# A two-layer hybrid decoder step: layer 1's rotations made in layer 0, short caches copied by sequence, load buffers by last use

## The chip, the cores and the metric

The kernel runs on 1 core of one Trainium2 chip. The metric is the device time of one execution in microseconds (us), lower is better. Before the change it is 2431.61 us, the median of 3 runs (2431.44 to 2434.77).

## The reference, cut to what matters

The reference is one inference step of two layers for a prompt of 512 positions and 8 sample sequences of 8 positions (T = 576 columns in all), with a model width of 1024, in float32. In each layer one projection of the normed input feeds four token mixers: A, dilated sliding-window attention in three head groups with caches of 128, 512 and 2048 positions (a1, a2, a3); B, grouped-query attention with a cache of 128 positions (b); C, a gated short convolution; D, a complex diagonal state-space layer. Their gated sum is projected, and a feed-forward part and a per-layer embedding follow. The outputs include the caches of the samples moved on by 8 positions, so that the old part of each cache is copied.

```python
a_bar = jnp.exp(lam * dt)                       # one complex number per state: a size and an angle
bu = jnp.einsum('blgi,gni->blgn', uf.astype(jnp.complex64), b_bar)
_, xs = lax.associative_scan(_ssm_combine, (a_seq, bu), axis=1)
y = jnp.einsum('blgn,gin->blgi', xs, c_mat).real + lp['ssm_d'].astype(f32) * uf
...
fk = jnp.concatenate([cache[2 * g].astype(ka.dtype), ka[:, :, g]], axis=1)
new += [last_rows(fk, lb), last_rows(fv, lb)]
```

## The kernel before, in words

Activations lie with channels on the 128 partitions and the 576 columns in two halves of 288. Each weight block of 128x512 (636 in all, 318 a layer, in the order of use) is loaded by SP's queue into one of 4 raw buffers (`wr`, `load_blk`, line 612), rounded by ScalarE to a high part (`wh`) and completed by GpSimd to a low part (`wl`, `split_blk`, line 617); 8 split blocks are held (NSPL, line 286). `gemms` (line 681) makes each product of three matmuls, so a block gives 4 x 2 x 3 = 24 matmuls of 128x288.

The program is written out by a planner in Python: `Build.track` (line 382) keeps a clock for each engine by its own costs, and every step of the main path lets side tasks (generators) go on when the planner thinks their inputs are there. The side tasks run in streams: state space, transposes of values, attention B, attention A, caches of the samples. The result is one fixed order for each engine, and each engine takes its instructions in order. The constants of this planner stand per layer in `PACE` (line 276): CALM is how far VectorE's clock may be ahead before a side task waits, BATCH after how many pieces side tasks are looked at, CONC how many tasks of a stream run at a time, PRE how many cache tiles are loaded ahead, MARGIN how many buffers stay free. Activations, loads and temporary data share 63 buffers of one size: `slot` (line 553) takes the one that was given back first, `drop` (line 558) gives it back. All profiled instructions bear line 256, that of the recording helper.

All transfers are issued by SP. The old cache parts are copied from DRAM to DRAM (`copies`, line 916; `after_step`, line 950, issues them evenly by count over the program): a1 in pieces of 2 sequences, a2 in halves of a sequence, a3 in eighths, b in pieces of 4 sequences (`COPY_PIECES`, line 33).

The state space has 8 blocks of 128 states. Its scan is made in real numbers: the input is turned back by the angle of its position, scanned with the size alone, and turned forward. The cosines and sines for 256 positions are doubled from 32: `ssm_setup` (line 1143) makes the 32 for all blocks and the output weights `ck`; `ssm_pair` (line 1464) loads the input weights (`bT`) and the inputs (`uscr`, a scratch in DRAM) of 2 blocks, doubles their 32 to 256 with 20 VectorE instructions, and scans two chunks of 256 positions. For layer 1, `ssm_setup` runs in layer 0's last steps. `sa_task` (line 1932) goes through the caches of 4 samples in 13 chunks, with tiles that `prefetch` (line 1959) loads ahead.

Of the kernel before, what the change touches and what calls it, by code (L numbers as in the profile page):

```python
# [19 lines left out]
L = 2  # L20
# [12 lines left out]
COPY_PIECES = {"a1": (2, 1), "a2": (1, 2), "a3": (1, 8), "b": (4, 1)}  # L33
# [234 lines left out]
def _free(ap):  # L268
    n = 1
    for st, c in list(ap.ap)[1:]:  # L270
# [6 lines left out]
    dict(CALM=5.12, ACALM=1.89, RES=4, LOBIAS=7.86, SLACK=-0.07, SIDE_MAX=4, MARGIN=0, PRE=6,  # L277
         CONC=(1, 3, 1, 2, 2), XCALM=0.3, SQP=-0.3, NEAR=-0.03, SCALM=4.55, SN=3, HOLD=False, BATCH=3, GR=2),
    dict(CALM=1.41, ACALM=0.0, RES=1, LOBIAS=14, SLACK=0.21, SIDE_MAX=3, MARGIN=3, PRE=8,
         CONC=(2, 4, 2, 2, 2), XCALM=0.3, SQP=0.23, NEAR=-0.6, SCALM=0, SN=5, HOLD=True, BATCH=1, GR=1),  # L280
)


class Build:
# [5 lines left out]
    ABIAS = 0.81  # L290
# [80 lines left out]
    def keys(self, ap):  # L371
# [4 lines left out]
        if nm in self.outer:  # L376
            return []
        if nm[:4] == "uscr":
            return [(nm, ap.offset // (128 * T))]
# [410 lines left out]
def build(nc, tc, A, stack):  # L790
# [7 lines left out]
    def load_x(src):  # L798
        xs = [B.slot() for _ in range(8)]
# [21 lines left out]
    def late_consts():  # L821
# [12 lines left out]
        [2, 4, 128, T], F32, name=f"uscr{l}") for l in range(L)]  # L834

# [307 lines left out]
    def ssm_setup(l, ssm):  # L1143
# [5 lines left out]
        Pc, Ps, Pn, kre, kim = ssm.Pc, ssm.Ps, ssm.Pn, ssm.kre, ssm.kim  # L1149
# [19 lines left out]
        yield from go()  # L1169

        cr = B.slot(shape=[128, 2, 8, 32])
# [15 lines left out]
        ssm.eb, ssm.ck = eb, ck  # L1187
# [21 lines left out]
    for l in range(L):  # L1209
# [76 lines left out]
        def ep_qkv(un, half, bk):  # L1286
            n, key = un.name, un.key
            c0, w = HS[half]
            if n in ("qa", "ka"):
# [5 lines left out]
                def go():  # L1295
# [3 lines left out]
                    if half == 1:  # L1299
# [4 lines left out]
                        P_.tensor_copy(t, s.t[:, 512:576])  # L1304
                        if n == "ka":
                            sync.dma_start(A["kvA"][l, 0, key[0], key[1]], s.t)
                        done.add((n, key))
# [156 lines left out]
        def ssm_pair(js):  # L1464
# [22 lines left out]
            for n, j in enumerate(js):  # L1487
                V.tensor_copy(es[n].t[:, :, 0:32], ssm.eb.t[:, :, j, :])
            for k in range(5, 8):
                w = 1 << k  # L1490
                yield from B.calm()
                for n, j in enumerate(js):
                    V.tensor_scalar(q[n].t[:, :, 0:w], es[n].t[:, :, 0:w], ssm.Pc[k][:, j:j + 1], None, op0=OP.mult)
                for i, f in ((0, ssm.Pn), (1, ssm.Ps)):
                    for n, j in enumerate(js):
                        V.scalar_tensor_tensor(es[n].t[:, i, w:2 * w], es[n].t[:, 1 - i, 0:w], f[k][:, j:j + 1],
                                               q[n].t[:, i, 0:w], op0=OP.mult, op1=OP.add)
# [5 lines left out]
            yield from B.wait(*[z_.t for z_ in bts + us])  # L1503
# [75 lines left out]
            if js[1] % 4 == 3:  # L1579
                while not all(("ssm", k) in done for k in range(4 * jj, 4 * jj + 4)):  # L1580
                    yield None
                ydp[jj] = B.slot()
# [7 lines left out]
        def ssm_sample(jj):  # L1590
# [5 lines left out]
            cr = B.slot(shape=[128, 2, 4, 32])  # L1596
# [70 lines left out]
            if all(("gelu", k) in done for k in range(2)):  # L1667
                B.drop(ssm.eb, ssm.ck)
# [181 lines left out]
        def sb_task():  # L1850
            kt = [B.slot(shape=[128, 4, 128]) for _ in range(2)]
            vt = [B.slot(shape=[128, 4, 128]) for _ in range(2)]
# [3 lines left out]
            mk = B.slot(BF, [128, 768])  # L1856
# [75 lines left out]
        def sa_task(qd):  # L1932
            if "mk" not in sam:
                sam["mk"] = [B.slot(BF, [128, 1152]), B.slot(BF, [128, 1024])]
# [24 lines left out]
            def prefetch():  # L1959
                while pos[0] < len(order) and len(tiles) < B.PRE:  # L1960
# [642 lines left out]
```

## Time and profile before

| | |
|---|---|
| median of 3 runs | 2431.61 us |
| the profiled execution | 2435.29 us, its span 2433.5 us |
| mean granted clock of TensorE | 0.981 of full speed |
| busy: PE, DVE, ACT, POOL | 2343.5, 1169.4, 992.8, 929.6 us |
| DMA | 358.95 MB in 163159 packets, mean 148 GB/s |

PE is TensorE's matmul, DVE is VectorE, ACT ScalarE, POOL GpSimd, SP the engine that issues the transfers. The profile is one execution on the hardware; its instruction groups carry the names of the program's buffers (s for the shared buffers, bk for accumulators in PSUM). The granted clock is given in shares of the full 2.4 GHz; the other level is 1.2 GHz. An idle time is put down to what ended it.

### The profile page before, as it was taken

To read this page: it belongs to the slowest core of one execution; us is meant where nothing else is said; L and a number is where in the kernel's file an instruction comes from. 1 tells how busy PE (TensorE), PEld (TensorE's weight loads), DVE (VectorE), ACT (ScalarE), POOL (GpSimd) and SP (SyncE) were. 2 spreads that over 40 slices of the span, in tenths; PEclk is the share of its full clock that TensorE was granted. 3 is DMA by queue.
4 is the path that set the end of the run, shared out by engine and by line. 5 is a ranking of instruction groups with operands and counts; after the bars stand their busy time and mean duration, and the time that the engine had idled before them with its cause. 6 is when DMAs were issued, how large, how long until landed. Compare 5 with 4: busy or idle time off the path is not lost.

```text
span 2433.5 us, 48402 instructions
## 1 busy us (share of the span) xinstructions
PE 2343.5 (96%) x18686; PEld 2239.5 (92%) x18686; DVE 1169.4 (48%) x3100; ACT 992.8 (41%) x2245; POOL 929.6 (38%) x947
## 2 busy tenths in 40 slices
PE   8899899999999999999997999999999999999999
PEld 8899688879999999999996989988789999999999
DVE  7976887432435210233647897565234342102343
ACT  4335456432455322334542346654233543223342
POOL 5346242223433433443232644423223344334432
PEclk9999899999999999999998999999999999999999
DMA  5345244874453344434453454534875433344322
GB/s 169 113 129 171 91 130 131 286 266 146 135 174 113 110 129 127 122 115 127 137 169 127 139 156 151 184 116 164 308 253 168 166 118 111 117 139 121 112 87 74
DMA packets 163159, 358.95 MB, mean 148 GB/s; under 512 B 24720, under 2 KB 33936, under 8 KB 157712
## 3 DMA queue, kind: packets, MB, share of 16 engines
q1 hardware_dynamic: 162928, 355.85, 45.9%
q8 instruction: 147, 2.41, 0.4%
q14 instruction: 84, 0.69, 0.1%
HBM read 331.59 MB, written 113.43 MB: 183 GB/s over the span
## 4 chain that ended last, share of the span: by engine, by line
PE 80%; DVE 11%; DMA 2%; ACT 2%; issue 2%; POOL 1%; SPq 1%; DVEq 0%; ACTq 0%; POOLq 0%
PE bk L256 80%; DVE s L256 8%; DVE bk L256 3%; DMA wr<-wblk 2%; ACT s L256 1%; SPq L256 1%; ACT wh L256 0%; DMA s<-cT 0%; POOL wl L256 0%; POOL s L256 0%; ACT zsw L256 0%; DVE bst L256 0%; DMA s<-kcA 0%; ACT bk L256 0%; ACT L256 0%
## 5 line engine op out<-in xcount | busy, mean ns | idle before, releaser
L256 PE MATMUL bk<-s,wh 128*128 128x288 f32 x10176 | 2077.1, 299 | 45.0 <-ACT s L256 19.8
L256 PEld LDWEIGHTS bk<-s,wh 128*128 128x128 f32 x10176 | 1644.1, 190 | 81.2 <-issue 25.3
L256 PE MATMUL bk<-s,wl 128*128 128x288 f32 x5088 | 1508.7, 297 | 0.5 <-POOL wl L256 0.5
L256 POOL TENSOR_TENSOR wl<-wr,wh 128x512 fp32r<-128x512 f32 x636 | 821.1, 1297 | 1422.0 <-ACT wh L256 1350.3
L256 PEld LDWEIGHTS bk<-s,wl 128*128 128x128 f32 x5088 | 964.6, 190 | 0.9 <-POOL wl L256 0.9
L256 DVE TENSOR_TENSOR bk<-bk,s 128x288 f32<-128x288 f32 (+2 forms) x620 | 288.6, 482 | 673.2 <-PE bk L256 643.2
L256 ACT ACTIVATE wh<-wr 128x512 fp32r<-128x512 f32 x636 | 398.9, 631 | 382.8 <-PE bk L256 243.8
L256 ACT ACTIVATE s<-bk 128x288 fp32r<-128x288 f32 (+5 forms) x456 | 181.4, 416 | 406.0 <-DVE bk L256 237.7
L256 PE MATMUL bk<-s,s 128*64 128x128 f32 (+8 forms) x2736 | 184.8, 319 | 20.1 <-DVE s L256 14.8
L256 ACT ACTIVATE zsw<-bk 32x288 f32<-32x288 f32 (+1 forms) x360 | 144.7, 403 | 132.6 <-DVE bk L256 89.0
L256 PEld LDWEIGHTS bk<-s,s 128*32 128x32 f32 (+4 forms) x2736 | 110.6, 130 | 71.9 <-issue 44.3
L256 ACT ACTIVATE rc<-bk 128x288 f32<-128x288 f32 x128 | 52.4, 409 | 236.1 <-DVE bk L256 235.2
L256 DVE TENSOR_TENSOR s<-s,bk 128x288 f32<-128x288 f32 (+1 forms) x226 | 95.1, 440 | 92.0 <-ACT bk L256 89.2
L256 DVE SCALAR_TENSOR_TENSOR s<-bk,s 128x288 fp32r<-128x288 f32 (+1 forms) x184 | 83.4, 456 | 74.1 <-ACT s L256 73.2
L256 PE MATMUL bk<-ident,s 128*128 128x128 f32 (+1 forms) x406 | 61.9, 285 | 16.8 <-ACT s L256 8.8
L256 DVE TENSOR_TENSOR s<-bk,s 128x512 f32<-128x512 f32 (+3 forms) x124 | 66.1, 572 | 23.9 <-PE bk L256 23.7
L256 DVE SCALAR_TENSOR_TENSOR bk<-rc,bk 128x288 f32<-128x288 f32 x96 | 44.2, 460 | 66.5 <-PE bk L256 34.8
L256 PEld LDWEIGHTS bk<-ident,s 128*128 128x128 f32 (+1 forms) x406 | 46.6, 141 | 27.4 <-issue 11.7
L256 DVE TENSOR_TENSOR s<-s,s 128x32 f32<-128x32 f32 (+8 forms) x221 | 68.6, 351 | 4.0 <-ACT s L256 1.2
L256 ACT ACTIVATE s<-bk,par 128x288 fp32r<-128x288 f32 (+1 forms) x80 | 41.3, 517 | 59.4 <-PE bk L256 43.5
L256 DVE COPY s<-bk 128x512 f32<-128x512 f32 (+6 forms) x80 | 35.8, 451 | 55.8 <-PE bk L256 38.7
L256 ACT ACTIVATE s<-s,bst 128x256 f32<-128x256 f32 (+1 forms) x83 | 38.6, 475 | 49.6 <-DVE bst L256 49.6
(113 smaller groups left out, 972.7 us busy)
## 6 DMA issues: line engine op xcount, KB each, us to landing
wr<-wblk SPq DMA_DIRECT2D x636, 256.0 KB, 2.8
old_a_k<-cache_a_k SPq DMA_DIRECT2D x128, 255.0 KB, 3.3
old_a_v<-cache_a_v SPq DMA_DIRECT2D x128, 255.0 KB, 3.3
s<-kcA SPq DMA_DIRECT2D x104, 256.0 KB, 5.4
s<-vcA SPq DMA_DIRECT2D x104, 256.0 KB, 5.2
old_a_k<-cache_a_k SPq DMA_DIRECT2D x32, 252.0 KB, 3.8
old_a_v<-cache_a_v SPq DMA_DIRECT2D x32, 252.0 KB, 3.5
kvA<-s SPq DMA_DIRECT2D x24, 288.0 KB, 2.1
```

The lines of the kernel that those rows point to most:

```text
L256: r = f(*a, **k)
```

## The change

1. a1's and b's old caches are copied in pieces of one sequence: 32 transfers of 120 KB for 16 of 240, and 32 of 60 KB for 8 of 240.
2. `doubled` is the doubling of `ssm_pair`, as a function. `ssm_turns`, a side task that is queued at the first step of layer 0's second feed-forward chunk, makes the 32 positions for layer 1 (`ssm_powers`), doubles all 8 blocks and writes them to a scratch in DRAM (`escr`, 8 x 256 KB). In layer 1, `ssm_pair` loads them instead of doubling.
3. `dslot` takes, for data that is loaded, the free buffer that the planner thinks was used last the longest ago. All loads into shared buffers but the first use it.
4. `sa_task` loads a tile ahead only when such a buffer is idle or soon will be, and asks again (`need`) before it uses one. The new key and value of a group are written out ahead of the copy of its last 64 columns.
5. The planner's constants of both layers change.

```diff
-COPY_PIECES = {"a1": (2, 1), "a2": (1, 2), "a3": (1, 8), "b": (4, 1)}
+COPY_PIECES = {"a1": (1, 1), "a2": (1, 2), "a3": (1, 8), "b": (1, 1)}
...
-    dict(CALM=5.12, ACALM=1.89, RES=4, LOBIAS=7.86, SLACK=-0.07, SIDE_MAX=4, MARGIN=0, PRE=6,
-         CONC=(1, 3, 1, 2, 2), XCALM=0.3, SQP=-0.3, NEAR=-0.03, SCALM=4.55, SN=3, HOLD=False, BATCH=3, GR=2),
-    dict(CALM=1.41, ACALM=0.0, RES=1, LOBIAS=14, SLACK=0.21, SIDE_MAX=3, MARGIN=3, PRE=8,
-         CONC=(2, 4, 2, 2, 2), XCALM=0.3, SQP=0.23, NEAR=-0.6, SCALM=0, SN=5, HOLD=True, BATCH=1, GR=1),
+    dict(CALM=3.77, ACALM=1.89, RES=4, LOBIAS=14, SLACK=-0.07, SIDE_MAX=4, MARGIN=2, PRE=6,
+         CONC=(1, 3, 1, 2, 2), XCALM=0.3, SQP=-0.3, NEAR=-0.03, SCALM=4.82, SN=5, HOLD=False, BATCH=1, GR=2),
+    dict(CALM=1.41, ACALM=0, RES=1, LOBIAS=12.4, SLACK=0.21, SIDE_MAX=3, MARGIN=3, PRE=10,
+         CONC=(2, 4, 2, 3, 1), XCALM=0.3, SQP=-0.3, NEAR=-0.6, SCALM=0, SN=2, HOLD=True, BATCH=1, GR=1),
...
-    ABIAS = 0.81
+    ABIAS = 0.18
...
+    def idle_at(self, i):
+        return self.last.get(self.ring.get(("s", i)), 0.0)
+
+    def dslot(self, dt=F32, shape=None):
+
+        i = min(self.free, key=self.idle_at)
+        self.free.remove(i)
+        self.free.appendleft(i)
+        return self.slot(dt, shape)
+
```

```diff
+    def doubled(js, ssm, es, q):
+
+        for n, j in enumerate(js):
+            V.tensor_copy(es[n].t[:, :, 0:32], ssm.eb.t[:, :, j, :])
+        for k in range(5, 8):
+            w = 1 << k
+            yield from B.calm()
+            for n, j in enumerate(js):
+                V.tensor_scalar(q[n].t[:, :, 0:w], es[n].t[:, :, 0:w], ssm.Pc[k][:, j:j + 1], None, op0=OP.mult)
+            for i, f in ((0, ssm.Pn), (1, ssm.Ps)):
+                for n, j in enumerate(js):
+                    V.scalar_tensor_tensor(es[n].t[:, i, w:2 * w], es[n].t[:, 1 - i, 0:w], f[k][:, j:j + 1],
+                                           q[n].t[:, i, 0:w], op0=OP.mult, op1=OP.add)
+
+    def ssm_turns(ssm):
+
+        yield from ssm_powers(ssm)
+        for j in range(0, 8, 2):
+            es, q = ([B.slot(shape=[128, 2, 256]) for _ in range(2)] for _ in range(2))
+            yield from doubled((j, j + 1), ssm, es, q)
+            yield from B.wait(*[z_.t for z_ in es])
+            for n in range(2):
+                B.side_dma(escr[j + n], es[n].t)
+            B.drop(*es, *q)
+        B.drop(ssm.eb)
+
+    def ssm_powers(ssm):
         VQ, go = on_v()
 
...
-        Pc, Ps, Pn, kre, kim = ssm.Pc, ssm.Ps, ssm.Pn, ssm.kre, ssm.kim
+        Pc, Ps = ssm.Pc, ssm.Ps
...
-        cr = B.slot(shape=[128, 2, 8, 32])
+        B.drop(*sq_)
+        ssm.eb = eb
+
+    def ssm_setup(l, ssm):
+        VQ, go = on_v()
+
+        def tt(out, a, b, op):
+            VQ.tensor_tensor(out, a, b, op)
+
+        kre, kim = ssm.kre, ssm.kim
+        if not l:
+            yield from ssm_powers(ssm)
+        sq_ = [B.slot(), B.slot()]
+        q1, q2 = sq_[0].t, sq_[1].t
+
+        cr = B.dslot(shape=[128, 2, 8, 32])
         B.side_dma(cr.t, A["cT"][l])
```

```diff
-            brs = [B.slot(shape=[128, 2, 128]) for _ in js]
-            urs = [B.slot() for _ in js]
+            brs = [B.dslot(shape=[128, 2, 128]) for _ in js]
+            urs = [B.dslot() for _ in js]
...
+            es = [B.dslot(shape=[128, 2, 256]) for _ in js] if l else []
+            for z_, j in zip(es, js):
+                B.side_dma(z_.t, escr[j])
...
-            es = [B.slot(shape=[128, 2, 256]) for _ in js]
+            if not l:
+                es = [B.slot(shape=[128, 2, 256]) for _ in js]
             q = [B.slot(shape=[128, 2, 256]) for _ in js]
-            yield from B.calm()
...
+            if not l:
                 yield from B.calm()
...
+                yield from doubled(js, ssm, es, q)
...
-            yield from B.wait(*[z_.t for z_ in bts + us])
+            yield from B.wait(*[z_.t for z_ in bts + us + es])
```

```diff
-                while pos[0] < len(order) and len(tiles) < B.PRE:
+                while pos[0] < len(order) and len(tiles) < max(B.PRE, 2 * B.GR) and B.free:
+                    at = min(B.idle_at(i_) for i_ in B.free)
+                    if at > B.now + 0.3:
+                        return at
                     kind, c, i = order[pos[0]]
-                    t_ = B.slot(shape=[128, 4, 128] if kind == "k" else [128, 2, 256])
...
+
+            def need(*keys):
+                while True:
+                    at = prefetch()
+                    if all(k_ in tiles for k_ in keys):
+                        break
+                    yield at
+                yield from B.wait(*[tiles[k_].t for k_ in keys])
 
...
                         once("A", lambda: (B.drain(has(("SA", 0), ("SA", 1), ("Afree", 1)), "SA"), B.room(4), split_a()))
                     if n == "fg" and un.key == CHUNKS[-1][0]:
                         once("p", load_p)
+                        if l + 1 < L:
+                            once("turns", lambda: B.task(ssm_turns(ssms[l + 1]), need=5))
                     if n == "dn" and un.key == (len(CHUNKS) - 1, 0):
                         once("psplit", split_p)
```

What moves in the order of the instructions, at three places. In the names, a buffer's letter is followed by a running number.

SP's queue at the start of layer 1, behind the state space's inputs (`uscr`); `wr` is a weight load, `bT` the input weights, `escr` the rotations. Before:

```order
L256 DMA s_15216<-bT 96x256
L256 DMA s_15218<-uscr_115 32x576 x3
L256 DMA s_15217<-bT 96x256
L256 DMA s_15219<-uscr_115 32x576 x3
L256 DMA old_a_k<-cache_a_k 2x2x15360 x2
L256 DMA wr_15268<-wblk 128x512
L256 DMA wr_15282<-wblk 128x512
L256 DMA old_a_v<-cache_a_v 2x2x15360 x2
L256 DMA wr_15383<-wblk 128x512
L256 DMA wr_15412<-wblk 128x512
L256 DMA old_a_v<-cache_a_v 2x2x15360 x2
L256 DMA old_a_k<-cache_a_k 16x4032
```

With the change:

```order
L256 DMA s_15351<-bT 96x256
L256 DMA s_15353<-uscr_115 32x576 x3
L256 DMA s_15352<-bT 96x256
L256 DMA s_15354<-uscr_115 32x576 x3
L256 DMA s_15363<-escr 128x512
L256 DMA s_15364<-escr 128x512
L256 DMA old_a_k<-cache_a_k 16x1920 x2
L256 DMA wr_15407<-wblk 128x512
L256 DMA wr_15421<-wblk 128x512
L256 DMA old_a_k<-cache_a_k 16x1920 x3
L256 DMA wr_15523<-wblk 128x512
L256 DMA wr_15550<-wblk 128x512
```

Four loads of rotations now stand ahead of the first weight load here (two in the rows shown, two further up behind the first pair's inputs), and a1's copies are twice as many, in 16 parts.

VectorE in layer 0, from the last instructions of the first feed-forward chunk to the first of the second; `s_9069` and `s_9085` are the norm's factor. Before:

```order
L256 TENSOR_TENSOR bk_11000<-bk_11000,zsw_11038 128x288
L256 SCALAR_TENSOR_TENSOR s_10966<-bk_11000,s_10965 128x288
L256 TENSOR_TENSOR bk_11826<-bk_11826,s_9069 128x288
L256 TENSOR_TENSOR bk_11855<-bk_11855,s_9069 128x288
L256 TENSOR_TENSOR bk_11855<-bk_11855,zsw_11881 128x288
L256 SCALAR_TENSOR_TENSOR s_11885<-bk_11855,s_11884 128x288
```

With the change, the end of the third pair of rotations and the start of the fourth:

```order
L256 TENSOR_SCALAR s_11980<-s_11978,s_248 128x2x128
L256 TENSOR_SCALAR s_11981<-s_11979,s_248 128x2x128
L256 SCALAR_TENSOR_TENSOR s_11978<-s_11978,s_248,s_11980 128x128
L256 SCALAR_TENSOR_TENSOR s_11979<-s_11979,s_248,s_11981 128x128
L256 SCALAR_TENSOR_TENSOR s_11978<-s_11978,s_248,s_11980 128x128
L256 SCALAR_TENSOR_TENSOR s_11979<-s_11979,s_248,s_11981 128x128
L256 TENSOR_TENSOR bk_11846<-bk_11846,s_9085 128x288
L256 TENSOR_TENSOR bk_11960<-bk_11960,s_9085 128x288
L256 COPY s_12046<-s_11852 128x2x32
L256 COPY s_12047<-s_11852 128x2x32
L256 TENSOR_SCALAR s_12048<-s_12046,s_248 128x2x32
L256 TENSOR_SCALAR s_12049<-s_12047,s_248 128x2x32
```

80 instructions of the rotations stand here that were in layer 1; two of the second chunk's come between the third and the fourth pair.

VectorE in layer 1, the third pair of blocks. Before, the end of the doubling and what follows it:

```order
L256 SCALAR_TENSOR_TENSOR s_16580<-s_16580,s_245,s_16582 128x64
L256 SCALAR_TENSOR_TENSOR s_16581<-s_16581,s_245,s_16583 128x64
L256 TENSOR_SCALAR s_16582<-s_16580,s_245 128x2x128
L256 TENSOR_SCALAR s_16583<-s_16581,s_245 128x2x128
L256 SCALAR_TENSOR_TENSOR s_16580<-s_16580,s_245,s_16582 128x128
L256 SCALAR_TENSOR_TENSOR s_16581<-s_16581,s_245,s_16583 128x128
L256 SCALAR_TENSOR_TENSOR s_16580<-s_16580,s_245,s_16582 128x128
L256 SCALAR_TENSOR_TENSOR s_16581<-s_16581,s_245,s_16583 128x128
L256 TENSOR_TENSOR bk_16549<-bk_16549,s_14098 128x288
L256 TENSOR_TENSOR s_16498<-s_16391,s_16498 32x256
L256 TENSOR_TENSOR s_16576<-s_16392,s_16576 32x256
L256 SCALAR_TENSOR_TENSOR s_16547<-rc_16618,bk_16610 128x288
```

With the change, the same place:

```order
L256 TENSOR_TENSOR bk_16460<-bk_16460,s_14261 128x288
L256 SCALAR_TENSOR_TENSOR s_16533<-rc_16531,bk_16515 128x288
L256 TENSOR_TENSOR bk_16535<-bk_16535,s_14261 128x288
L256 SCALAR_TENSOR_TENSOR s_16533<-rc_16581,bk_16573 128x288
L256 TENSOR_TENSOR bk_16589<-bk_16589,s_14261 128x288
L256 SCALAR_TENSOR_TENSOR s_16648<-rc_16646,bk_16630 128x288
L256 TENSOR_TENSOR s_16596<-s_16485,s_16596 32x256
L256 TENSOR_TENSOR s_16671<-s_16486,s_16671 32x256
L256 TENSOR_TENSOR s_16675<-bk_16708,s_16497 128x512
L256 TENSOR_TENSOR s_16676<-bk_16709,s_16498 128x512
L256 TENSOR_TENSOR bk_16708<-bk_16708,s_16497 128x512
L256 TENSOR_TENSOR bk_16709<-bk_16709,s_16498 128x512
```

The doubling is gone, and the 32x256 instructions, which complete the input weights, follow the gates' work.

## Rows read from the trace of the kernel before

**Rows 1.** The page: span, PE's busy time, and the clock in 40 slices of the span.

```profile
span 2433.5 us, 48402 instructions
...
PE 2343.5 (96%) x18686; PEld 2239.5 (92%) x18686; DVE 1169.4 (48%) x3100; ACT 992.8 (41%) x2245; POOL 929.6 (38%) x947
...
PEclk9999899999999999999998999999999999999999
```

**Rows 2.** Stretches: stretch, its length, each engine's busy us (instructions), clock, DMA share, GB/s.

```profile
230.00:370.00 140.00, 122.35 (x975) 111.59 (x974) 117.22 (x347) 74.45 (x170) 50.09 (x51) 0.90 0.39 119
760.00:1145.00 385.00, 385.00 (x2909) 384.98 (x2907) 90.67 (x195) 123.42 (x247) 151.77 (x119) 1.00 0.40 122
1145.00:1230.00 85.00, 79.25 (x578) 77.39 (x577) 56.18 (x149) 51.80 (x124) 31.16 (x25) 0.98 0.46 138
1230.00:1340.00 110.00, 94.43 (x657) 90.43 (x656) 66.18 (x169) 32.23 (x67) 34.59 (x32) 0.91 0.46 149
1340.00:1510.00 170.00, 164.29 (x1283) 155.69 (x1282) 147.40 (x395) 80.31 (x178) 90.65 (x138) 0.99 0.49 151
```

**Rows 3.** PE's waits in 1230 to 1340 us: for whom, total us, times, longest.

```profile
PE bk L256 <- ACT s L256: 14.4, 3, 7.0
```

**Rows 4.** Timeline, ACT and PE: start, us, instruction, [idle before <-releaser].

```profile
1296.86 0.63 ACT L256 ACTIVATE wh<-wr 128x512 fp32r<-128x512 f32 x1 [7.17 <-DMA wr<-wblk]
...
1297.84 1.10 PE L256 MATMUL bk<-s,wh 128*128 128x288 f32 x2 [7.03 <-ACT s L256]
...
1307.84 0.63 ACT L256 ACTIVATE wh<-wr 128x512 fp32r<-128x512 f32 x1 [8.65 <-DMA wr<-wblk]
...
1309.98 0.85 PE L256 MATMUL bk<-s,wh 128*128 128x288 f32 x2 [6.70 <-ACT s L256]
```

**Rows 5.** DMA issues (KB, median us to landing); the chain; a1's landing from 1230 to 1300.

```profile
wr<-wblk SPq DMA_DIRECT2D x636, 256.0 KB, 2.8
old_a_k<-cache_a_k SPq DMA_DIRECT2D x128, 255.0 KB, 3.3
...
1288.51 19.22 DMA wr<-wblk
...
DMA to landing us min/median/max: 20.7/20.7/20.7
```

**Rows 6.** Stretches around the two waits, columns as in rows 2.

```profile
1265.00:1275.00 10.00, 10.00 (x78) 10.00 (x77) 6.69 (x20) 2.25 (x4) 2.58 (x2) 1.00 0.68 221
1285.00:1297.00 12.00, 5.09 (x36) 4.44 (x34) 5.34 (x15) 3.35 (x8) 3.46 (x6) 0.89 0.32 114
1297.00:1310.00 13.00, 5.46 (x28) 5.03 (x28) 4.06 (x9) 4.33 (x12) 3.96 (x4) 0.76 0.38 121
1310.00:1320.00 10.00, 10.00 (x58) 9.74 (x59) 9.70 (x23) 4.38 (x8) 4.64 (x4) 0.76 0.45 158
```

**Rows 7.** Timeline of SP's queue: start, us to issue, what.

```profile
1270.13 0.43 SPq L256 DMA_DIRECT2D s<-bT  x1
...
1286.40 0.57 SPq L256 DMA_DIRECT2D old_a_k<-cache_a_k  x1
```

**Rows 8.** DVE's groups in 1268 to 1440 us: instruction xcount | busy us, mean ns.

```profile
L256 DVE SCALAR_TENSOR_TENSOR s<-s,s,s 128x32 f32<-128x32 f32 (+2 forms) x48 | 14.9, 369 | 0.0
...
L256 DVE TENSOR_SCALAR s<-s,s 128x64 f32<-128x64 f32 (+2 forms) x24 | 8.5, 395 | 0.0
...
L256 DVE COPY s<-s 128x64 f32<-128x64 f32 x8 | 1.2, 186 | 0.0
```

**Rows 9.** Stretches of layer 0's feed-forward part, columns as in rows 2.

```profile
940.00:960.00 20.00, 20.00 (x153) 20.00 (x153) 0.00 (x0) 5.97 (x12) 8.18 (x7) 1.00 0.41 131
960.00:980.00 20.00, 20.00 (x154) 20.00 (x153) 3.79 (x9) 6.40 (x13) 10.29 (x8) 1.00 0.62 190
```

**Rows 10.** Timeline of PE: layer 0's two longest waits after the start.

```profile
269.68 1.12 PE L256 MATMUL bk<-ident,s 128*128 128x128 f32 x4 [5.73 <-ACT s L256]
...
344.31 1.30 PE L256 MATMUL bk<-ident,s 128*128 128x128 f32 x5 [5.18 <-DVE s L256]
```

More of the change, by code (lines that the diff above doesn't have):

```diff
@@ L377, in keys @@
             return []
+        if nm[:4] == "escr":
+            return [(nm, ap.offset // (128 * 512))]
         if nm[:4] == "uscr":
@@ L798, in load_x @@
     def load_x(src):
-        xs = [B.slot() for _ in range(8)]
+        xs = [B.dslot() for _ in range(8)]
         for m in range(8):
@@ L834, in build @@
         [2, 4, 128, T], F32, name=f"uscr{l}") for l in range(L)]
+    escr = stack.enter_context(tc.tile_pool(name="drame", bufs=1, space=bass.MemoryType.DRAM)).tile(
+        [8, 128, 2, 256], F32, name="escr")
     class Stat:
@@ L1186, in ssm_setup @@
         B.drop(*sq_, cr)
-        ssm.eb, ssm.ck = eb, ck
+        ssm.ck = ck
         ssm.bus = {}
@@ L1581, in ssm_pair @@
                     yield None
-                ydp[jj] = B.slot()
+                ydp[jj] = B.dslot()
                 B.side_dma(ydp[jj].t, uscr[l][jj, 3])
@@ L1595, in ssm_sample @@
             B.side_dma(x0, A["x0"][l, jj])
-            cr = B.slot(shape=[128, 2, 4, 32])
+            cr = B.dslot(shape=[128, 2, 4, 32])
             B.side_dma(cr.t, A["cT"][l][:, :, js, :])
@@ L1850, in sb_task @@
         def sb_task():
-            kt = [B.slot(shape=[128, 4, 128]) for _ in range(2)]
-            vt = [B.slot(shape=[128, 4, 128]) for _ in range(2)]
+            kt = [B.dslot(shape=[128, 4, 128]) for _ in range(2)]
+            vt = [B.dslot(shape=[128, 4, 128]) for _ in range(2)]
             for i in range(2):
@@ L1959, in prefetch @@
             def prefetch():
-                while pos[0] < len(order) and len(tiles) < B.PRE:
+                while pos[0] < len(order) and len(tiles) < max(B.PRE, 2 * B.GR) and B.free:
+                    at = min(B.idle_at(i_) for i_ in B.free)
+                    if at > B.now + 0.3:
+                        return at
                     kind, c, i = order[pos[0]]
-                    t_ = B.slot(shape=[128, 4, 128] if kind == "k" else [128, 2, 256])
+                    t_ = B.dslot(shape=[128, 4, 128] if kind == "k" else [128, 2, 256])
                     B.side_dma(t_.t, A["kcA" if kind == "k" else "vcA"][l, qd, c, i])
@@ L1973, in sa_task @@
                     if n % B.GR == 0:
-                        yield from B.wait(qq[0].t, qq[1].t, *[
-                            tiles["k", c_, i].t for c_ in cs[n:n + B.GR] for i in range(2)])
+                        yield from B.wait(qq[0].t, qq[1].t)
+                        yield from need(*[("k", c_, i) for c_ in cs[n:n + B.GR] for i in range(2)])
                     for hp in range(2):
@@ L2040, in sa_task @@
                     if n % B.GR == 0:
-                        yield from B.wait(pt.t, *[tiles["v", c_, i].t for c_ in cs[n:n + B.GR] for i in range(2)])
+                        yield from B.wait(pt.t)
+                        yield from need(*[("v", c_, i) for c_ in cs[n:n + B.GR] for i in range(2)])
                     for b in range(4):
@@ L2362, in build @@
         for k in "CS":
-            ropeT[k] = B.slot()
+            ropeT[k] = B.dslot()
             B.side_dma(ropeT[k].t, A["rope" + k])
```

21 lines of the change are left out of this document (5 added, 16 removed).

## The prediction

> **What bounds the kernel now.** I read the page first, then the stretches, then the waits of TensorE (PE). On the page [rows 1] PE is busy 2343.5 of 2433.5 us, and every instruction of the change stands on other engines or in queues. So PE's work of 2343.5 us stays, and only what is not work can go: some 90 us of gaps, and the time in which PE was granted 1.2 instead of 2.4 GHz. The strip of the clock shows where: a digit below 9 (half level in part of a slice) stands behind a gap, not by itself. The table by stretches [rows 2] puts the gaps in three places. 230 to 370 us, layer 0's attention beside its state space, lacks 140 - 122.35 = 17.65 us at a mean clock of 0.90, with VectorE (DVE) busy 117 of 140. 1230 to 1340, the start of layer 1, lacks 15.6 us at 0.91, though DVE is busy 66 of 110 only. 1340 to 1510, layer 1's state space, lacks 5.7 at 0.99, with DVE at 147 of 170. In 760 to 1145, layer 0's feed-forward part, PE has no gap and DVE is busy 90.67 of 385.
>
> **Part 1, the copies of the short caches.** The waits of 1230 to 1340 are nearly one kind: 14.4 us on ScalarE (ACT) in 3 waits [rows 3]. The timeline shows two of 7.03 and 6.70 us, and ahead of each an ACT that stood still for a weight load (7.17 and 8.65 us) and then made the operand that PE lacked [rows 4]. ACT takes its instructions in order, so a late weight load holds back whatever is queued behind the rounding of that load. The weight load on the chain there took 19.22 us, where the 636 of them have a median of 2.8; the one piece of a1 with a measured landing in the same stretch took 20.7, while 128 pieces of a3, which are larger, land in 3.3 [rows 5]. While this goes on the 16 DMA engines are busy 0.32 and 0.38 of the time, at 114 and 121 GB/s; ten microseconds earlier they moved 221 [rows 6]. So not the amount is late. A transfer that spreads over all engines ends with the slowest of them, and a few are held. The order names the candidates: a1's pieces go out as 2x2x15360 elements, b's as 4x15360, and the a2 and a3 pieces, which land fast, as 16 parts of about 4,000. The change makes them 16x1920 and 16x960, the shape of the fast ones.
>
> What it is worth: the two gaps, 13.7 us. Behind them PE ran at the half level: 58 matmuls in the 10 us from 1310 and 28 in 5.46 busy us from 1297, against 78 in 10 us at full level [rows 6]. That is (78 - 58) x 0.128 = 2.6 and 28 x (0.195 - 0.128) = 1.9 us. Together 18.2; I take **-18**. Bounds: 0 if the amount was it after all, -18.2 if both go entirely. I stay near the upper end, since the two rows of DMA share are far from a full queue. The price: 40 more issues by SP, 0.43 to 0.57 us each [rows 7], in a queue that mostly waits for free weight buffers; nothing on the path.
>
> The Trainium skill, "DMA: Bandwidth & Descriptors", section "Rules for kernel authors", speaks against this edit: many small transfers are to be coalesced into a large one, and under 64 KB one pays mostly overhead. By it alone, pieces of 120 and 60 KB in place of 240 give the queue more to do, part 1 is worth nothing, and the sum below is -7. In this trace 255 KB in 16 parts landed six times faster than 240 KB in few, so here I let the spread decide and not the size.
>
> **Part 2, the rotations leave layer 1.** In each of layer 1's four pairs 2 copies, 6 multiplications and 12 fused operations leave DVE. In 1268 to 1440 us these are 8, 24 and 48 instructions: 1.2 + 8.5 + 14.9 = 24.6 us [rows 8]. PE's gaps in 1340 to 1510 are 5.7 us, and 1% of clock, 1.7. DVE is off the path in most of the stretch, so at most 7.4 come back. And PE arrives earlier once part 1's gaps are gone: DVE has 18 us less to do the same work, which uses up much of the 24.6. I take **-3** (bounds 0 and -7.4). The powers of the rotation, which layer 0's last steps now make for layer 1, go too: PE's gaps in 1145 to 1230 are 5.75 us [rows 2], mostly the change to the next part; I take **-1** (0 to -3).
>
> They arrive in layer 0's down projection. By the order, three pairs stand there back to back (60 DVE instructions) and the fourth behind two feed-forward instructions. At 24.6 / 4 = 6.15 us a pair this is 18.5 us in one go. It begins where DVE is busy 0.00 of 20 us, and the next 20 us hold 9 feed-forward instructions [rows 9]. Those wait up to some 15 us, while PE goes on into free accumulators. I take **0**, because PE has no gap in the 385 us; if the cover is gone (all accumulators full) it costs up to +5.
>
> **Part 3, the reloads.** Eight 256 KB writes there, 8 reads in layer 1. Of the reads 4 stand in SP's queue ahead of the first weight load behind the state space's transfers. SP issues a load in about 0.43 us [rows 7], so that load goes out 1.7 us later, behind 1.05 MB more, 4.7 us at 221 GB/s [rows 6]. What hides it: eight blocks are split ahead, each used by 24 matmuls, 8 x 24 x 0.128 = 25 us. I take **0**; without cover +6.4 and the clock behind it. The buffer choice by last use only moves which buffer a load takes; SP's place in the order stays, 0.
>
> **Part 4, the pace of layer 0.** The wait of 5.73 us at 263.9 is a transposition whose softmax stands on DVE behind the state space's operations [rows 10]. The planner let DVE run 5.12 ahead there; now 3.77, and it looks at the side work after every piece, not after each third. A backlog smaller by 1.35 in the two waits of over 5 us in layer 0 (5.73, and 5.18 likewise) gives 2.7 us. In the order the same work is only spread: ScalarE, GpSimd and DVE change by 1 to 5 instructions of a form. Bounds: as good as layer 1's stretch (5.7 of 170 us for 17.65 of 140: -13 and the clock, -20 in all), or three more such waits with their clock, +18. I take **-3**. Layer 1's second cache task now follows the first; 1660 to 1760 is covered by matmuls: 0.
>
> **Sum.** -18 - 3 - 1 + 0 + 0 - 3 = -25 on the profiled execution's 2435.29: 2410.3. The median of the runs shown, 2431.61, stands 3.7 lower, so I predict **2407 us** (2406.6), and 0.2% (4.9 us, about what a measurement of this kernel tells from no change) means 2426.7 to 2436.5.
>
> **Rivals.**
> - Layer 0's stretch becomes like layer 1's. For it: the same tasks, and layer 1 already looks after every piece with a backlog of 1.41. Against: its DVE load was 117 of 140. -18 - 4 - 17 = -39: 2393.
> - Part 1's gaps go and come again elsewhere: every wait of layer 0 is laid anew, and DVE must do layer 1's work in less time. Half to all of the 25 given back: 2419 to 2432.
> - No gain from the copies, by the amount of bytes (the rule above): the weight loads wait for the 2.3 MB of state-space writes and their reads before them. For it: those transfers moved at 221 GB/s just before. Against: DMA share 0.32 in the wait. -7: 2425.
> - **Slower**: the same, and the rotation loads are the last straw. Their place is ahead of the weight load after the state space's transfers; price 6.4 us on the first gap, about 5 on the second load's queue, and 4 of clock: +15 - 7 = +8, 2440. It decides from the point where that load lands over 25 us after the last split block was begun, that is if a1's pieces still land near 20 us in 16 parts.
>
> **How the numbers follow.** Forecast (2396 to 2419) 0.58; layer 0 like layer 1 (2388 to 2396) 0.14; given back 0.14, of it half within 0.2%; no gain from the copies 0.06, half within 0.2%; slower 0.08. Faster by over 0.2%: 0.58 + 0.14 + 0.07 + 0.03 = 0.82; within: 0.10; slower: 0.08. The range 2390 to 2428 leaves out the best of layer 0 and all beyond an even result; about 8 in 10 remain.
>
> **What would show it.** Right: no wait of ACT over 3 us on a weight load in layer 1's first 100 us; weight loads there at most 7 us to landing, a1's pieces under 6; clock 1.0 in that stretch; no rotation among layer 1's DVE groups, and 24 to 25 us more DVE busy around 960 to 1000 with PE still without a gap. Wrong: a weight load over 10 us behind the rotation loads, PE waiting for DVE in the down projection, or layer 0's 230 to 370 us with more than 18 us of gaps, which would outweigh the rest.

## The result and the profile after

The changed kernel takes **2395.15 us** (median of 4 runs, 2389.81 to 2397.03), against 2431.53 for the kernel before (4 runs) on the same chip: a ratio of 0.9844, 95% interval 0.9826 to 0.9862. That is 36.4 us less. The forecast was 2407 us, 24.6 less; the time lies inside the range, and the gain is half as large again as forecast.

The page of the changed kernel's profiled execution (2397.03 us), to be read beside [rows 1]:

```profile
span 2395.2 us, 48488 instructions
...
PE 2328.1 (97%) x18686; PEld 2227.9 (93%) x18686; DVE 1171.4 (49%) x3105; ACT 990.7 (41%) x2245; POOL 923.1 (39%) x942
...
PEclk9999999999999999999999999999999999999999
```

PE runs the same 18686 matmuls. Its busy time fell by 15.4 us although no matmul went, since it ran less at the half level; the rest of the 38.3 us between the two spans is idle time that went. DVE's busy time did not fall: the work was moved.

The stretches of [rows 2] in the changed kernel (the same columns; the program is 7 to 11 us ahead of the kernel before in the second and third, 10 to 41 in the last two):

```profile
230.00:370.00 140.00, 123.94 (x1021) 113.11 (x1019) 126.15 (x360) 78.25 (x191) 51.60 (x53) 0.95 0.43 135
760.00:1145.00 385.00, 384.87 (x2907) 384.64 (x2907) 119.12 (x309) 125.01 (x255) 155.14 (x121) 1.00 0.42 130
1145.00:1230.00 85.00, 80.73 (x593) 78.89 (x592) 48.86 (x115) 52.71 (x125) 29.95 (x24) 0.98 0.42 127
1230.00:1340.00 110.00, 108.66 (x815) 104.99 (x814) 79.59 (x178) 33.20 (x70) 46.32 (x59) 1.00 0.51 158
1340.00:1510.00 170.00, 167.71 (x1405) 159.61 (x1404) 127.68 (x354) 93.20 (x208) 86.49 (x120) 1.00 0.55 175
```

The fourth row is the largest: at layer 1's start PE lacked 15.6 of 110 us before and lacks 1.3 now, at full clock. In the second row DVE has 28.45 us more than before, and PE lacks 0.13 of 385.

Fixed stretches shift against each other, so the next table goes by work: both kernels run the same 15264 matmuls of weights (10176 with `wh`, 5088 with `wl`) in the same order, and each row is the time from the start of one of them to the start of another, read from the two traces.

| matmuls of weights | part | before, us | after, us | difference | forecast |
|---|---|---|---|---|---|
| 0 to 2880 | layer 0's mixers | 573.3 | 565.1 | -8.2 | -3 |
| 2880 to 7440 | layer 0's projections and most of its feed-forward part | 624.6 | 623.9 | -0.7 | 0 |
| 7440 to 7920 | change to layer 1 | 69.1 | 67.1 | -2.0 | -1 |
| 7920 to 8160 | layer 1's start, with the two long waits | 53.8 | 36.7 | -17.1 | -18 |
| 8160 to 9600 | layer 1's state space | 234.8 | 225.7 | -9.1 | -3 |
| 9600 to the last | the rest | 868.2 | 867.0 | -1.2 | 0 |

The places are those of the forecast. Whether the causes are, the experiments tell. The first row depends on the clock of one place near 500 us: two executions with the same order of instructions give -8.2 and -14.5 there (last section).

PE's waits from 1230 to 1340 us in the changed kernel (for whom, total, times, longest), in place of [rows 3]:

```profile
PE bk L256 <- DVE s L256: 1.3, 1, 1.3
```

The weight loads' landing from 1255 to 1300 us, in place of the 19.22 of [rows 5]:

```profile
DMA to landing us min/median/max: 2.5/3.3/4.6
```

The rotations' transfers among the DMA issues (KB, median us to landing):

```profile
escr<-s SPq DMA_DIRECT2D x8, 256.0 KB, 2.3
s<-escr SPq DMA_DIRECT2D x8, 256.0 KB, 3.2
```

No wait for ACT is left, no weight load takes 5 us, and the reloads land as fast as a weight load. The rotations arrive where the forecast put them, in the stretches of [rows 9] and the two behind:

```profile
940.00:960.00 20.00, 20.00 (x153) 20.00 (x152) 8.53 (x23) 5.21 (x10) 7.88 (x6) 1.00 0.47 135
960.00:980.00 20.00, 20.00 (x153) 20.00 (x152) 19.35 (x69) 3.91 (x9) 5.14 (x4) 1.00 0.58 199
980.00:1000.00 20.00, 20.00 (x153) 20.00 (x152) 6.30 (x14) 7.68 (x16) 10.21 (x8) 1.00 0.56 184
```

DVE is full for 20 us and PE does not miss a moment.

### The profile page after: what moved, and what is told of

The parts are those of the page before. It is cut to its first block, busy times and chain, and to the rows that moved or that the text cites. A ratio compares the mean times of both kernels' runs of the same rounds, so it can differ in the third digit from the quotient of the medians.

```text
span 2395.2 us, 48488 instructions
## 1 busy us (share of the span) xinstructions
PE 2328.1 (97%) x18686; PEld 2227.9 (93%) x18686; DVE 1171.4 (49%) x3105; ACT 990.7 (41%) x2245; POOL 923.1 (39%) x942
## 4 chain that ended last, share of the span: by engine, by line
PE 83%; DVE 10%; ACT 2%; DMA 2%; issue 1%; POOL 1%; SPq 0%; DVEq 0%; ACTq 0%; POOLq 0%
PE bk L256 83%; DVE s L256 7%; DVE bk L256 3%; ACT s L256 1%; POOL s L256 1%; POOL wl L256 1%; DMA s<-kcA 0%; DMA wr<-wblk 0%; SPq L256 0%; ACT wh L256 0%; ACT L256 0%; DMA s<-vcA 0%; ACT zsw L256 0%; ACT bk L256 0%; DMA s<-uscr 0%
## 5 line engine op out<-in xcount | busy, mean ns | idle before, releaser
L256 ACT ACTIVATE s<-bk 128x288 fp32r<-128x288 f32 (+3 forms) x454 | 179.9, 415 | 390.5 <-DVE bk L256 234.4
L256 PE MATMUL bk<-s,s 128*32 128x128 f32 (+10 forms) x2736 | 180.5, 315 | 11.9 <-DVE s L256 5.4
L256 PEld LDWEIGHTS bk<-s,s 128*32 128x32 f32 (+5 forms) x2736 | 108.9, 129 | 60.3 <-issue 33.5
```

What stands on the lines that cost most here:

```text
L256: r = f(*a, **k)
```

## The experiments

All medians; each kernel ran beside the kernel before (2430.8 to 2431.7), and the ratio is to that. In the columns behind the name, "old" and "new" stand for the copies, for where the rotations are made, and for layer 0's row of planner constants. In "all but the copies" the old pieces go out at the places that the change gives them, further apart than in the kernel before.

| kernel | copies | rotations | layer 0's row | us | ratio, 95% interval |
|---|---|---|---|---|---|
| before | old | old | old | 2431.5 | 1 |
| copies alone, pieces of 1 sequence | new | old | old | 2423.47 | 0.9966 [0.9953, 0.9979] |
| copies alone, old pieces in 16 parts | 16 parts | old | old | 2419.8 | 0.9952 [0.9936, 0.9968] |
| rotations alone | old | new | old | 2431.05 | 0.9999 [0.9990, 1.0008] |
| layer 0's row alone | old | old | new | 2424.2 | 0.9974 [0.9962, 0.9986] |
| all but the copies | old | new | new | 2404.13 | 0.9895 [0.9883, 0.9908] |
| all but the rotations | new | old | new | 2412.96 | 0.9924 [0.9911, 0.9936] |
| all but layer 0's row | new | new | old | 2406.34 | 0.9901 [0.9886, 0.9916] |
| changed | new | new | new | 2395.15 | 0.9844 [0.9826, 0.9862] |

### The copies: size or spread

The first four keep the order of all instructions of PE, DVE, ACT and POOL as it was; only the form or the number of the copies in SP's queue differs.

**Copies alone, one sequence at a time**, in the kernel before (the planner is told of the old piece):

```diff
-yield lambda ...: sync.dma_start(
-    o[l, b:b + nb, ...], a[l, b:b + nb, ...])
+for s in range(nb):
+    sync.eng.dma_start(o[s:s + 1], a[s:s + 1])
+B.track("Q", "dma_start", (o, a), {})
```

> The kernel before, with the order of every instruction of every engine kept; only the copies of a1 and b go out one sequence at a time, at the places of the old pieces. Theory A (spread: a piece in few long parts sits on few DMA engines, and a weight load, which needs all engines, ends with the slowest): the two waits at layer 1's start go, 17 to 18 us with their clock, some 2414 us. Theory B (size: what helps is that a transfer is half as large): the same, 2414. Theory C (the waits at layer 1's start went because the rotations left that place, or with the new order): nothing, 2431.

Measured: 2423.47 us, 8 us less, not 18. PE's waits from 1225 to 1345 us:

```profile
PE bk L256 <- DVE s L256: 8.1, 3, 4.8
PE bk L256 <- ACT rc L256: 0.4, 1, 0.4
```

The landing of the weight loads from 1260 to 1312:

```profile
DMA to landing us min/median/max: 2.5/3.8/4.9
```

The loads are mended and the wait for ACT is gone, but a new wait of 4.8 us for DVE stands in its place. DVE's timeline there (start, us, instruction) shows what it did:

```profile
1287.89 1.40 DVE L256 COPY s<-s 128x64 f32<-128x64 f32 x2
1289.21 1.47 DVE L256 TENSOR_SCALAR s<-s,s 128x64 f32<-128x64 f32 x2
1290.60 0.73 DVE L256 SCALAR_TENSOR_TENSOR s<-s,s,s 128x32 f32<-128x32 f32 x4
1291.25 0.47 DVE L256 TENSOR_SCALAR s<-s,s 128x128 f32<-128x128 f32 x2
1291.64 0.86 DVE L256 SCALAR_TENSOR_TENSOR s<-s,s,s 128x64 f32<-128x64 f32 x4
1292.42 0.95 DVE L256 TENSOR_TENSOR bk<-bk,s 128x288 f32<-128x288 f32 x2
```

The last row is the product of the main path that ACT, and behind it PE, waited for. Ahead of it in DVE's queue stands the doubling of a pair. While the loads were late, that was hidden under their wait.

**Old pieces in 16 parts.** The same bytes in the same transfers, with another order of the dimensions (a1: 8x2x3840 for 2x2x15360; b: 4x4x3840 for 4x15360, so that only a1's outermost dimension grows):

```diff
-sync.dma_start(o[l, b:b + nb, ...], a[l, b:b + nb, ...])
+v = [t.rearrange("b (p r) d -> p b (r d)", p=16 // nb) for t in (o, a)]
+sync.eng.dma_start(*v)
```

> The kernel before, order kept; the pieces keep their size (a1 2 sequences, b 4 sequences) and their places, but their elements are written down in 16 parts of 3,840 instead of 4 of 15,360. Theory A (spread): as good as pieces of one sequence, some 2414 us, and the one a1 piece at layer 1's start lands in under 7 us instead of 20.7. Theory B (size): nothing, 2431 us. Theory C: nothing, 2431 us.

Measured: 2419.8 us. The wait for ACT is gone too (waits for DVE: 5.5 us in 3). Size is not it.

What landed in 20.7 us in the kernel before is not a piece of a1, though [rows 5], the prediction and this expectation call it one. The kernel before, 1230 to 1312 us:

```profile
old_a_k<-cache_a_k SPq DMA_DIRECT2D x4, 252.0 KB, 12.3
old_a_k<-cache_a_k SPq DMA_DIRECT2D x4, 240.0 KB
```

The pieces of 240 KB, a1's, have no measured landing. The two measured ones are of 252 KB, a2's, in 16 parts: the first, issued at 1286.40 us right behind a1's last, took 20.7 us, and a later one 3.9. With a1 in 16 parts, a2's first lands in 7.6. So a transfer in 16 parts is slow where it stands behind a1's few long ones.

**The changed kernel with the old pieces**, issued at the place of the first of them (`nb` is 2 for a1, 4 for b):

```diff
-sync.dma_start(o[l, b:b + 1, ...], a[l, b:b + 1, ...])
+if b % nb == 0:
+    sync.eng.dma_start(o[b:b + nb, ...], a[b:b + nb, ...])
```

> The changed kernel, order kept; the copies of a1 and b go out as before, 2 and 4 sequences in one transfer, at the place of the first of them. Theory A and B: the waits at layer 1's start come back, 14 to 18 us, some 2411 us, with a weight load there that takes over 15 us. Theory C: nothing, 2395 us.

**The changed kernel with a1's pieces of 120 KB in 2 parts** (2x15360 for 16x1920):

```diff
-COPY_PIECES = {"a1": (1, 1), ...}
+COPY_PIECES = {"a1": (2, 2), ...}
```

> The changed kernel, order kept; a1 is copied in the same number of pieces of the same 120 KB at the same places, but a piece is half of 2 sequences, that is 2 parts of 15,360 elements instead of 16 of 1,920. Theory A (spread): the slow landings come back, and with them most of the waits at layer 1's start, 8 to 17 us, 2403 to 2412 us. Theory B (size): nothing, 2395 us. Theory C: nothing, 2395 us.

Measured: 2404.13 and 2404.73 us, 9 to 10 us more than the changed kernel, both with PE's wait for ACT back. The waits from 1225 to 1345 us, of the first and of the second:

```profile
PE bk L256 <- ACT s L256: 6.8, 1, 6.8
```

```profile
PE bk L256 <- ACT s L256: 7.5, 1, 7.5
```

Half the size in few parts is as bad as the whole size in few parts. By work, both lose 9.3 to 9.8 us between matmuls 7920 and 8160, where the changed kernel had gained 17.1. So at that place the form of the copies is worth at least 9 of the 17 once the rotations are gone, and 11 to 12 (the two kernels with the copies alone, by the same count) while they are still there. The 9 is not the price of the old copies as they were: the change also puts a1's pieces further apart. From layer 1's first matmuls on, 1.44 MB of a1 (six old pieces) are issued within 29 and 35 us in these two kernels, and within 12 us (1273.91 to 1285.74) in the kernel before. The old pieces in the old rhythm were not tried in the changed kernel.

**The changed kernel with 240 KB in 16 parts**, the second form above on the changed kernel:

> The changed kernel, order kept; a1 and b go out in transfers of 240 KB again (40 issues fewer), written down in 16 parts of 3,840 elements. If spread alone counts: 2395 us, within 0.2%, and possibly a few us better than the changed kernel for the issues that are saved; if size counts: 2404 us.

Measured: 2396.13 us, ratio 0.9855 [0.9843, 0.9868]: the same as the changed kernel. 40 issues fewer are worth nothing, as 40 more cost nothing.

### The rotations

**All but the rotations.** Layer 1 doubles for itself again:

```diff
-es = [B.dslot(shape=[128, 2, 256]) for _ in js] if l else []
-for z_, j in zip(es, js):
-    B.side_dma(z_.t, escr[j])
...
-if not l:
-    yield from doubled(js, ssm, es, q)
+yield from doubled(js, ssm, es, q)
...
-once("turns", lambda: B.task(ssm_turns(ssms[l + 1]), need=5))
```

> The changed kernel without the move of the rotations: layer 1 makes its 32 positions in layer 0's last steps and doubles them in its four pairs, as before; copies, paces and buffers as changed. Theory A (the prediction's price): 3 us for the doubling in the pairs and 1 for the powers, 2399 us. Theory B (formed from the wait of 4.76 us that stayed when only the copies were changed: the doubling of a pair stands on DVE ahead of a gate's product that PE waits for, and four pairs do so): 4.8 us and its clock at layer 1's start, 7 us behind it, 2 ahead of it, some 2410 us. Theory C (the doubling is hidden): 2395.

Measured: 2412.96 us, 17.8 more than the changed kernel: more than theory B gave, and over four times the prediction's price. PE's waits from 1225 to 1345 us are for DVE again:

```profile
PE bk L256 <- DVE s L256: 5.2, 2, 4.2
```

By work it loses 9 us from matmul 7680 to 8400 and 11 from 8640 to 9360. Undoing the move lets the planner lay layer 1 anew, so the next kernel does it with the order kept.

**The work twice.** The changed kernel, with 80 instructions as in `doubled`, on the spare buffers `q`, at the old places in layer 1:

```diff
+else:
+    V.eng.tensor_copy(q[n].t[:, :, 0:32], ssm.ck.t[:, :, j, :])
+    for k in range(5, 8):
+        V.eng.tensor_scalar(...)
+        V.eng.scalar_tensor_tensor(...)
```

> The changed kernel, order kept, with the 80 doubling instructions of layer 1 made once more on DVE at the places where they stood before; their result goes into spare buffers and is not used. Theory A (the prediction's price: DVE is off the path there): 3 us, 2398. Theory B (DVE takes its instructions in order, and the doubling stands ahead of gates' products that PE's accumulators wait for): most of the 17.8 us that undoing the move cost, 2407 to 2413. Theory C (what the move gained came from the order, the buffers or the powers, not from DVE's time): under 2 us, 2395 to 2397.

Measured: 2417.22 us, ratio 0.9944 [0.9932, 0.9956], 22 us more than the changed kernel. The rotations still come from DRAM, and copies, buffers and order are the same, so these 22 us come from the 80 instructions on DVE alone. The 20 of a pair stand in one run here; in the kernel before, products of the main path stand between them in three of the four pairs, so the old layout's own price may differ. PE's waits, from 1225 to 1345 and from 1345 to 1450 us; in the changed kernel they are 1.3, and 2.3 us from 1330 to 1450:

```profile
PE bk L256 <- DVE s L256: 7.4, 1, 7.4
...
PE bk L256 <- DVE s L256: 12.2, 5, 4.7
```

There are three waits of over 4 us (7.4, 4.3, 4.7). Ahead of each DVE makes the 20 instructions of a pair: in the first with a product of the main path behind them, in the two others with the 32x256 instructions that complete the input weights of the pair's own matmuls.

**The rotations alone**, in the kernel before (layer 1's `ssm_pair` loads, `ssm_turns` writes; all else as before):

```diff
+once("turns", lambda: B.task(ssm_turns(ssms[l + 1]), need=5))
...
+for z_, j in zip(es, js):
+    B.side_dma(z_.t, escr[j])
```

> The kernel before with the move of the rotations alone (made and written in layer 0, loaded in layer 1); copies, paces, buffers and the caches' loading as before. Theory A (the prediction's price): 4 us, 2427. Theory B (the move is worth the same whatever the copies do): 17.8 us, 2413. Theory C (at layer 1's start the late weight loads still hold PE, so the move gains there only what is behind them): 8 to 13 us, 2418 to 2423.

Measured: 2431.05 us, ratio 0.9999 [0.9990, 1.0008]: nothing, less than any theory gave. PE's waits from 1225 to 1345 us, then the weight load on the chain of waits, and the PE row of the timeline that it ends in:

```profile
PE bk L256 <- ACT s L256: 16.3, 2, 13.4
```

```profile
1291.04 19.25 DMA wr<-wblk
```

```profile
1313.09 0.85 PE L256 MATMUL bk<-s,wh 128*128 128x288 f32 x2 [13.42 <-ACT s L256]
```

With DVE's work gone, the late weight loads are the whole wait: 16.3 us against 14.4 of [rows 3], with two weight loads on the chain one after the other, of 11.15 and 19.25 us. They are as slow as in the kernel before (11.04 and 19.22), but the second was issued 2.5 us later (1291.04 against 1288.51 us), behind the loads of rotations. By work, the stretch from 7920 to 8160 is 3.9 us longer than in the kernel before. From 8160 to 8880 the rotations alone gain 10.8 us, as much as in the changed kernel (10.5); a few are lost behind. This fits the mechanism of the rival that ended slower (rotation loads ahead of weight loads, while a1's pieces hold the queue); its price at that place was 4 us, not 15.

### Layer 0's pace, and what was priced at nothing

**Layer 0's row alone**, in the kernel before, and **all but layer 0's row**:

```diff
-dict(CALM=5.12, LOBIAS=7.86, MARGIN=0, SCALM=4.55, SN=3, BATCH=3, ...),
+dict(CALM=3.77, LOBIAS=14, MARGIN=2, SCALM=4.82, SN=5, BATCH=1, ...),
```

> The kernel before with layer 0's row of planner constants as changed, nothing else. Theory A (the row is worth what layer 0 lost with the old one in the changed kernel): 8 to 11 us shorter, all of it ahead of 600 us, some 2421. Theory B (the row fits the changed kernel's buffers only): 0 or slower, 2431 or more.

> The changed kernel with layer 0's row of planner constants as before. Layer 0 was 8.3 us shorter in the changed kernel up to its feed-forward part. Theory A (the smaller backlog and the look after every piece did it): 6 to 8 us come back there, some 2402 us. Theory B (the loads' buffers and the caches' asking for idle ones did it): nothing in layer 0, 2395. Theory C (any new order of layer 0 gives another few us of either sign): something between 2385 and 2415 with waits at other places than in either kernel.

Measured: 2424.2 us for the first, 7.5 less than before; 2406.34 for the second, 11.2 more than the changed kernel. By work both differences lie ahead of matmul 2880 (-12.7 and +8.1 in the profiled executions), and behind it no stretch moves by over 1.6 us. PE's waits from 225 to 370 us, of the row alone and of all but the row:

```profile
PE bk L256 <- DVE s L256: 9.0, 7, 2.6
PE bk L256 <- ACT s L256: 7.0, 2, 4.2
```

```profile
PE bk L256 <- DVE s L256: 12.3, 7, 5.1
PE bk L256 <- ACT s L256: 7.3, 3, 5.7
```

The first pair is, to the digit, that of the changed kernel; the second has about the 5.73 and 5.18 of [rows 10]. So the row makes layer 0's gain. The sum of these waits fell by 2 to 4 us only, and part of the gain is clock. Of the 12.6 us between matmuls 0 and 2880 that the row alone gained, 4.6 are PE's idle time and 8.0 its busy time, with the same number of matmuls. Of the 8.0 that the old row costs in the changed kernel, 6.6 are idle and 1.4 busy, but against an execution of the changed kernel that had itself lost time at the half level near 500 us. The stretch 262 to 284 us, before and in the changed kernel:

```profile
262.00:284.00 22.00, 15.06 (x112) 11.19 (x110) 17.50 (x56) 8.67 (x20) 2.02 (x2) 0.69 0.23 70
```

```profile
262.00:284.00 22.00, 18.39 (x194) 15.11 (x193) 19.79 (x60) 10.99 (x27) 4.61 (x6) 1.00 0.40 116
```

With the wait of 5.73 us in it the stretch was granted 0.69 on the mean; with one of 2.64 us at the same place, the full clock.

**The buffers of the loads**, order kept:

```diff
 def dslot(self, dt=F32, shape=None):
-    i = min(self.free, key=self.idle_at)
-    self.free.remove(i)
-    self.free.appendleft(i)
     return self.slot(dt, shape)
```

> The changed kernel with the order of every instruction of every engine kept; only the buffer that a load takes is again the one given back first, not the one used last the longest ago. Theory A (the prediction: worth 0): 2395 us, within 0.2%. Theory B (a load waits in the queue for the last reader of its buffer, and the loads behind it with it): 3 to 10 us longer, mostly where the caches of the samples are read (240 to 520 and 1440 to 1760 us).

Measured: 2399.02 us, ratio 0.9862 [0.9848, 0.9876]. The interval overlaps that of the changed kernel, and the profiled execution, at 2392.11, was shorter than the changed kernel's; by work no stretch is longer by over 1.4 us. A gain of a few us from `dslot` is neither shown nor excluded.

**Layer 1's row as before**:

```diff
-dict(LOBIAS=12.4, PRE=10, CONC=(2, 4, 2, 3, 1), SQP=-0.3, SN=2, ...),
+dict(LOBIAS=14, PRE=8, CONC=(2, 4, 2, 2, 2), SQP=0.23, SN=5, ...),
```

> The changed kernel with layer 1's row of planner constants as before. Theory A (the prediction gave this row nothing): 2395 us. Theory B (8.5 us that layer 1 gained between its start and its feed-forward part came from the row, not from the rotations): 5 to 8 us longer, 2400 to 2403, without any change ahead of layer 1.

Measured: 2394.03 us, ratio 0.9847 [0.9834, 0.9861]: the row is worth nothing, as priced. No kernel tried is shown to be faster than the changed one. Not tried by themselves are `need` and the new condition of `prefetch`, the earlier writing of the new keys and values, and `ABIAS`.

## Why the prediction was right, and where its terms were not

**The sum held for a reason that it did not state.** One part alone gives 8 to 11.5 (copies), 0 (rotations) and 7.5 us (row): 15.5 to 19 together. Taken out of the changed kernel they cost 9 to 10, 17.8 and 11.2: 38 or more. The whole gives 36.4. That the second sum comes near it is in part chance, since the copies' 9 is for pieces that stand further apart than the old ones did. Copies and rotations stand on the same path at layer 1's start: PE waits for an ACT held by a late load, and with that wait gone, for a DVE held by the doubling (4.8 us with the copies alone); with the doubling gone, the late load holds PE at least as long as before. With both gone 1.3 us are left. The kernel before with these two parts and nothing else was not run; the nearest, all but layer 0's row, takes 24.5 us less, where the two alone give 8 and 0.

**Part 1, -18.** What the load waits for was right: the parts of the copies, not the amount of bytes. a1 in 16 parts is fast at 240 KB and at 120 KB, and slow in few parts at either size. One reading on the way was wrong: the 20.7 us belong to a2's first piece, of 252 KB in 16 parts, so "six times faster" compares 16 parts with 16 parts, and no trace has a landing of a 240 KB piece. The conclusion held, as the runs with 16 parts show. The step that failed is "the two gaps, 13.7 us": it took both to go whole, with no second wait behind them, and the copies alone gave 8 to 11.5; the place gave its 17.1 only with the rotations gone too. The Trainium skill, "DMA: Bandwidth & Descriptors", section "Rules for kernel authors", wants small transfers made into large ones; here 240 and 120 KB in 16 parts are the same (2396.13 and 2395.15 us). The row of the same table of the Trainium skill on using all 16 engines, by which the outermost dimension sets how many engines a transfer is spread over, is the one that the runs bear out: 2x2x15360 and 2x15360 are slow, 8x2x3840 and 16x1920 are not.

**Part 2, -3 and -1.** The step that failed is "DVE is off the path in most of the stretch, so at most 7.4 come back". DVE was busy 147 of 170 us there, but the price is set by what stands behind 20 instructions in its queue at four places: the work left in layer 1 cost 17.8 us, and put back on top, in one run a pair, 22. The sentence after it had the clue and drew the wrong conclusion: that PE arrives 18 us earlier, with the same work for DVE to do, makes that work more costly and its removal worth more. The arrival in the down projection, 0, was right: 28.45 us more of DVE (24.6 were forecast) under a PE without a gap. So was the change to layer 1 (-2.0 for -1).

**Part 3, 0.** Right with the new copies: reads of rotations land in 3.2 us and no weight load behind them takes 5. With the old copies alone it was not: layer 1's start took 3.9 us more, with the late weight load 2.5 us later.

**Part 4, -3.** Mis-sized: 7.5 to 11.2. The waits' sum became smaller by about what was said (18.0 to 16.0 us from 225 to 370 us, the longest now 4.2); the term left out the clock, though [rows 2] had it, with 0.90, and PE's busy time fell by 8.0 us with the row alone. The prediction had counted the clock only in the bound.

**Rivals.** No row of the table by work gave anything back. The time lies just outside the forecast's own band (2396 to 2419) and in that of the rival in which layer 0 becomes like layer 1 (2388 to 2396, chance 0.14), but did not come by it: layer 0 still lacks 16.1 of 140 us.

## What to carry to other kernels

Before pricing a wait that is to go, look at what the waiting place would wait for next: read what each engine has queued between the end of the removed wait's cause and the instruction that PE needs. Two causes that cover each other look worth little one by one and are worth more together than their two gains, so they are tried as a pair, and taken out of the pair one at a time. When a part is taken out again, look whether its rhythm in the queue comes back with it. A copy beside a stream of loads is to be written with a large outermost dimension: here 8 and 16 did well and 2 did not, at 120 and at 240 KB.

## What the runs showed of the hardware

- **Few long parts, one after another.** By the trace's packet records, in the kernel before, copies of a1 and b make 96 packets of 61,440 bytes, median 2.27 us. Around the two long waits a1's go in twos, each two right behind the last but for two gaps of 1.3 us, from 1275.4 to 1306.1 us, while the engines as a whole are busy 0.32 to 0.38 [rows 6]. Of the 16 packets of a2's piece of 20.7 us, 14 start from 1287.8 to 1288.3 us and the other two at 1306.0 and 1306.1, when a1's last two end. So a few engines were held, as the prediction had it, and here they were two. As 8x2x3840 the same bytes are 384 packets of 15,360 bytes, median 0.57 us.
- **DVE beside POOL.** In the kernel with the work twice, by forms, from 1264 to 1282 us:

```profile
L1558 DVE SCALAR_TENSOR_TENSOR s<-s,s 128x32 f32<-128x32 f32 x4 | 3.9, 1038 | 0.0
...
L1558 DVE SCALAR_TENSOR_TENSOR s<-s,s 128x64 f32<-128x64 f32 x4 | 0.9, 270 | 0.0
```

The smaller form took 1038 ns, the one with twice the elements 270. Through the first, POOL was completing weight blocks (four in 5.06 us from 1269.52); through the second it was idle. At 1349.00 us the four of 128x64 took 2.98 us, beside two such completions (2.50 us from 1349.41), against 0.86 here. So the price of DVE's work in layer 1 depends on what POOL does beside it. Whether POOL was the cause was not tried by itself. The Trainium skill, "GPSIMD Engine Reference", names in section "Specifications" a contention with DVE's instructions that have two SBUF inputs, as these do; the rows agree with it.
- **The clock at one place differs between runs.** Stretch 498 to 518 us, the changed kernel and the one without `dslot`, whose engines have the same order:

```profile
498.00:518.00 20.00, 17.95 (x181) 15.50 (x180) 8.37 (x16) 5.65 (x11) 4.91 (x8) 0.74 0.54 185
```

```profile
498.00:518.00 20.00, 18.15 (x237) 15.96 (x238) 9.52 (x19) 5.17 (x10) 5.22 (x5) 1.00 0.78 268
```

About the same busy time, at 0.74 and at 1.00. By work (matmuls 2400 to 2640) this place makes 4.9 us between the two profiled executions, as much as the bound below which the prediction called two times the same. Of the changed kernel's four runs the longest (2397.03 us) had the lowest mean clock, 0.989, and the shortest (2389.81) the highest, 0.993. So layer 0's gain in the table by work, -8.2 us, is that of an execution which lost time here; the kernel without `dslot` has -14.5 in its place.
